# All experts for 512 tokens instead of 448, the fourth block's sums through one PSUM bank

## The chip, the cores and the metric

The kernel runs on one core of one Trainium2 chip. The time is device microseconds (us) of one execution; the figure for the kernel before is the median of 3 runs. The engines spoken of are PE (TensorE), DVE (VectorE), ACT (ScalarE), POOL (GpSimd, which here issues the gathering DMAs) and SP (SyncE, which issues all other DMAs).

## The reference, cut to what matters

One encoder layer for 1024 tokens of width 1024, all in float32: norm, two attentions, a merge, and then `peer`, a layer of 16384 one-neuron experts of which each token takes 16 in each of 8 heads. Only `peer` is touched by the change.

```python
s1 = jnp.einsum('thd,hnd->thn', q[:, :, 0], keys[:, 0])
s2 = jnp.einsum('thd,hnd->thn', q[:, :, 1], keys[:, 1])
v1, i1 = lax.top_k(s1, PEER_TOPK)          # 16 of 128
v2, i2 = lax.top_k(s2, PEER_TOPK)
cand = v1[..., :, None] + v2[..., None, :] # 256 sums, the best 16 are the token's experts
sc, ci = lax.top_k(cand, PEER_TOPK)
e = i1[ci // 16] * PEER_NKEYS + i2[ci % 16]
g = jax.nn.softmax(sc, axis=-1)
hid = jnp.einsum('thkd,td->thk', u[e], xb)
a = jax.nn.gelu(hid, approximate=False) * g
out = jnp.einsum('thk,thkd->td', a, v[e])
```

## The kernel before

The 1024 tokens are eight blocks of 128. Everything ahead of `peer` runs block by block on PE with its helpers: projections, attentions, `merge` (branches, output projection, residual, second norm, the scores q and the top 16 of each half, done by `top16` on DVE), and `choose` (the 16 best pairs of each head, on DVE with some copies on ACT).

The experts are computed in one of two ways. **Gathered**, for blocks 0, 1, the first half of 2, and 6, 7 (`GATHER`, function `experts`, L772 to L817): POOL issues for each of 128 choices of a token one indirect DMA that brings a row of u (128 tokens, 512 KB); DVE multiplies and sums it (L803); then the same with v, where DVE multiplies and adds (L809). Of the half block each token's 128 choices lie on two partitions, so that 64 + 64 DMAs do it instead of 128 + 128. **Dense**, for blocks 3, 4, 5 and the second half of 2 (`DENSE`, function `dense_experts`, L672 to L763): all 16384 experts at 448 tokens, in 128 chunks of 128 experts. The weight of an expert at a token, zero for nearly all, comes from `gates` (L633 to L670), which builds it on DVE, ACT and PE, four tokens a step, and writes it to DRAM, from where it is read back as `gj`.

In a chunk, PE makes `ph` (hidden values of 128 experts at 448 tokens) out of `ut` and the tokens `x2h`, `x2l`; float32 numbers are split into two float32r parts and multiplied in three products (`mm3`), so `ph` is 24 matmuls with 448 columns. ACT takes the Gelu, DVE multiplies by `gj` (L739), and `split` makes `ah`, `al` out of the first 384 tokens. One chunk later `second` adds up `v` times these: 18 matmuls with 512 columns into six PSUM banks, three blocks by two column halves, which stay open over all 128 chunks (L701). The half block goes unsplit, in plain float32, into a seventh bank: two matmuls (L704), which the profile lists as four. `ph` has the eighth bank. So all eight PSUM banks are taken.

What sets the order: the code emits instructions in a program order, and a scheduler that simulates the program gives each engine a fixed list. What is emitted early has priority. `experts` is emitted last, so gathers fill what is left, from block 0's choice on until the end. A tile pool that is opened in place of closed ones waits for all that was still at work in them. `fstack` is a stack of pools that closes before `dense_experts`; the pools `yza` and `tkp`, in which `choose` works, are not in it (L81, L82) and stay open to the end. The pool `dk` of the dense stage (L676) takes the room of the closed ones.

The last lines before the dense stage give its surroundings; `sel` runs `choose` for two blocks:

```python
    weave(mop(2, mp, yzb), 26, (gates(gk, d1), 32 * len(d1)))
    weave(mop(3, mp, yza), 26, (chain(sel([4, 5], yzb), gates(gk, d2)), 18 + 32 * len(d2)))
run(sel([6, 7], yza))
fstack.close()
dense_experts()
for seg in GATHER:
    experts(*seg)
```

## Time and profile before

| what | value |
|---|---|
| median of 3 runs | 3414.91 us (3405.22 to 3427.95) |
| span of the profiled execution | 3413.5 us, from its first to its last instruction; 1.4 us under the median |
| PE busy | 3029.9 us (89%) |
| DVE busy | 2723.6 us (80%) |
| ACT busy | 1395.7 us (41%) |
| POOL busy | 1377.9 us (40%) |
| moved by DMA | 1047 MB, mean 307 GB/s |
| dense stage, first to last matmul | about 2064 to 3374 us |

The profiled execution has only its span as its own time; what lies around it in a run (1.4 us against the median) is taken as unchanged. Shares of the span mix stages with different limits, so each stage is read by itself: by the busy time of the engines in a stretch, by the order of the instructions on an engine, and by the chain of waits (the work that ended last, followed back from the end, each step to what released it).

### The profile page before, as it was taken

How to read it: one execution, taken by the hardware profiler on the slowest of the kernel's cores; microseconds unless marked ns; L12 is line 12 of the kernel's file. 1: busy time of each engine (PE TensorE's matmuls, PEld its weight loads, DVE VectorE, ACT ScalarE, POOL GpSimd, SP SyncE). 2: the span in 40 equal slices, each digit the busy share in tenths (PEclk: the TensorE clock that was granted, in tenths of full speed). 3: DMA queues.
4: the chain of work that ended last, by engine and by line, in shares of the span. 5: the costliest groups of instructions: out<-in, count | busy, mean ns of one | idle time of the engine just before them, and what ended most of it. 6: DMA issues, size and time to landing. Idle time of an engine off the chain costs nothing.

```text
span 3413.5 us, 47714 instructions
## 1 busy us (share of the span) xinstructions
PE 3029.9 (89%) x15648; PEld 2435.4 (71%) x15648; DVE 2723.6 (80%) x5871; ACT 1395.7 (41%) x2959; POOL 1377.9 (40%) x1156
## 2 busy tenths in 40 slices
PE   7997689999979988888766658999999999999995
PEld 7986578888857656567655656777777777777774
DVE  4435798777759999988899898888788878788887
ACT  6633433443324554438505864333333333333332
POOL 0000445554534442343334421554444545445554
PEclk9998899999989988899887878999999999999997
DMA  7775989999989997788888877999999999999997
GB/s 240 215 243 169 357 313 356 345 330 337 323 322 350 329 321 233 227 281 309 328 288 303 319 250 242 347 339 333 329 336 333 333 340 329 331 332 329 330 331 269
DMA packets 415960, 1047.19 MB, mean 307 GB/s; under 512 B 44640, under 2 KB 181664, under 8 KB 413792
## 3 DMA queue, kind: packets, MB, share of 16 engines
q0 software_dynamic: 165888, 604.05, 50.3%
q1 hardware_dynamic: 249824, 440.09, 37.3%
q8 instruction: 123, 2.02, 0.2%
q14 instruction: 125, 1.02, 0.1%
HBM read 969.43 MB, written 73.96 MB: 306 GB/s over the span
## 4 chain that ended last, share of the span: by engine, by line
PE 69%; DVE 12%; DMA 7%; issue 6%; ACT 5%; POOL 1%; SPq 0%; DVEq 0%; ACTq 0%; POOLq 0%
PE ph L136 18%; PE mm L136 15%; PE acc L701 15%; PE mm L480 7%; PE sc L344 4%; PE acc L704 4%; PE pv L362 3%; PE tr L203 2%; DVE junk L803 2%; PE gg L660 2%; DVE acc L809 1%; DMA ge<-in_u_dram,ei 1%; ACT gst L662 1%; ACT o L652 1%; DMA wr<-in_w_bd_dram 1%
## 5 line engine op out<-in xcount | busy, mean ns | idle before, releaser
L797 POOL DMA_INDIRECT ge<-in_u_dram,ei x512 | 610.1, 1192 | 1051.0 <-DVE junk L803 415.2
L797 POOL DMA_INDIRECT ge<-in_v_dram,ei x512 | 626.1, 1223 | 695.3 <-DVE acc L809 446.3
L809 DVE SCALAR_TENSOR_TENSOR acc<-ge,a,acc 128x1024 f32<-128x1024 f32 x576 | 736.4, 1279 | 11.1 <-DMA ge<-in_v_dram,ei 5.1
L803 DVE SCALAR_TENSOR_TENSOR junk<-ge,xs 128x1024 bf16<-128x1024 f32 x576 | 701.6, 1218 | 40.2 <-DMA ge<-in_u_dram,ei 33.8
L129 DVE TENSOR_TENSOR wl<-wr,wh 128x1024 fp32r<-128x1024 f32 x232 | 283.8, 1224 | 322.0 <-ACT wh L128 196.4
L128 ACT CAST wh<-wr 128x1024 fp32r<-128x1024 f32 x232 | 243.3, 1049 | 605.8 <-PE ph L136 432.4
L136 PE MATMUL ph<-x2h,wh 128*128 128x448 f32 x1024 | 388.8, 380 | 11.3 <-DVE x2l L129 9.2
L136 PE MATMUL mm<-xh,wh 128*128 128x256 f32 (+1 forms) x1248 | 374.6, 326 | 5.4 <-ACT wh L128 3.8
L136 PE MATMUL mm<-xl,wh 128*128 128x256 f32 (+1 forms) x1248 | 369.5, 322 | 7.7 <-DVE xl L232 7.7
L136 PE MATMUL ph<-x2l,wh 128*128 128x448 f32 x1024 | 375.2, 366 | 0.0
L136 PEld LDWEIGHTS ph<-x2h,wh 128*128 128x128 f32 x1024 | 192.2, 188 | 128.5 <-issue 57.6
L136 PEld LDWEIGHTS mm<-xh,wh 128*128 128x128 f32 x1248 | 238.2, 191 | 30.5 <-ACT st L286 4.1
L136 PEld LDWEIGHTS mm<-xl,wh 128*128 128x128 f32 x1248 | 237.8, 191 | 29.3 <-DVE xl L232 9.7
L136 PE MATMUL mm<-xh,wl 128*128 128x256 f32 (+1 forms) x1248 | 239.3, 327 | 0.3 <-DVE wl L129 0.3
L344 PE MATMUL sc<-kt,qt 64*128 64x256 f32 (+3 forms) x608 | 215.9, 522 | 24.8 <-DVE mn L346 12.6
L136 PE MATMUL ph<-x2h,wl 128*128 128x448 f32 x1024 | 229.8, 366 | 0.0
L136 PEld LDWEIGHTS ph<-x2h,wl 128*128 128x128 f32 x1024 | 191.7, 187 | 17.5
L136 PEld LDWEIGHTS ph<-x2l,wh 128*128 128x128 f32 x1024 | 192.7, 188 | 15.7
L136 PEld LDWEIGHTS mm<-xh,wl 128*128 128x128 f32 x1248 | 186.4, 191 | 18.4 <-issue 1.5
L701 PE MATMUL acc<-vh,ah 128*128 128x512 f32 x768 | 197.6, 392 | 0.0
L701 PE MATMUL acc<-vh,al 128*128 128x512 f32 x768 | 194.9, 389 | 0.0
L701 PE MATMUL acc<-vl,ah 128*128 128x512 f32 x768 | 194.9, 389 | 0.0
(197 smaller groups left out, 5258.3 us busy)
## 6 DMA issues: line engine op xcount, KB each, us to landing
vr<-in_v_dram SPq DMA_DIRECT2D x128, 512.0 KB
wr<-in_ut_dram SPq DMA_DIRECT2D x128, 512.0 KB
wr<-in_w_in_dram SPq DMA_DIRECT2D x104, 512.0 KB
gdr<-gst SPq DMA_DIRECT2D x14, 2048.0 KB
gj<-gdr SPq DMA_DIRECT2D x448, 64.0 KB
wr<-in_w_bd_dram SPq DMA_DIRECT2D x40, 512.0 KB
wr<-in_w_out_dram SPq DMA_DIRECT2D x40, 512.0 KB
wr<-in_wq_dram SPq DMA_DIRECT2D x40, 512.0 KB
```

The source lines that it names most:

```text
L128: nc.scalar.copy(hi, raw)
L129: nc.vector.tensor_sub(lo, raw, hi.bitcast(F32))
L136: nc.tensor.matmul(o, w[a][:, k, :], xx[b][:, k, :], start=(i == 0), stop=(i == last))
L203: nc.tensor.transpose(o[:, i * P:(i + 1) * P], s, ident)
L344: nc.tensor.matmul(o[:, :k1 - k0], q, k[:, k0:k1], start=True, stop=True)
L362: nc.tensor.matmul(o[:, :P], aT[:, j - c, :], vt[:, v0 + j, :], start=(j == 0), stop=(j == n - 1))
L480: nc.tensor.matmul(o, w[:, k, :], xx[:, k, :], start=(k == 0), stop=(k == K - 1))
L701: nc.tensor.matmul(acc[i][hf], a[x][:, i * P:(i + 1) * P], b[y][:, hf * 512:hf * 512 + 512], **kw)
L704: nc.tensor.matmul(acc4[hf * n4:(hf + 1) * n4], ge[:, 3 * P:], vr[:, hf * 512:hf * 512 + 512], start=(j == 0), stop=(j == NCH - 1))
L797: nc.gpsimd.indirect_dma_start(out=t, out_offset=None, in_=src, in_offset=bass.IndirectOffsetOnAxis(ap=ei[:, k:k + 1], axis=0))
L803: nc.vector.scalar_tensor_tensor(junk, t, 1.0, xs, op0=OP.mult, op1=OP.mult, accum_out=hid[:, k:k + 1])
L809: nc.vector.scalar_tensor_tensor(acc, t, a[:, k:k + 1], acc, op0=OP.mult, op1=OP.add)
```

## The change

The half block 2 of the dense stage becomes a whole one: blocks 2, 3, 4, 5 are dense (512 tokens), blocks 0, 1, 6, 7 are gathered. The code that handled parts of blocks goes.

- The gathers of the first half of block 2, 64 of u and 64 of v, go, with their DVE instructions. `gates` gets 16 more steps (128 instead of 112) and takes block 2 ahead of block 3.
- `ph`, Gelu, the multiplication by `gj` and `split` take 512 columns; `gj` is 16 DMAs for four chunks instead of 14.
- The two float32 matmuls of the half block go. In their place `fourth` adds up the fourth block (block 5) in the split form: for two chunks at a time, six matmuls with 512 columns for one column half in one PSUM bank (`acc3`), then an addition on DVE into `rest` in SBUF, which began as the block's residual. The other half uses the same bank, after `second` of the newer chunk. So every second chunk has on PE: `ph`, `fourth(0)`, `second`, `fourth(1)`; the others `ph`, `second`.
- Buffers: `vh`, `vl`, `ah`, `al` have 4 (of 3), `vr` 2 (of 3), `ge` 2 (of 3).
- The pools `yza` and `tkp` move into `fstack`, at the same place; so their room is given to `dk`.
- At the end, the residual of the third dense block is loaded into a buffer of `vr`.

Comments that the change only removes, and lines that follow from the new names, are left out:

```diff
--- before.py
+++ after.py
...
-DENSE = [(3, 0, 128), (4, 0, 128), (5, 0, 128), (2, 64, 128)]
-GATHER = [(0, 0, 128), (1, 0, 128), (2, 0, 64), (6, 0, 128), (7, 0, 128)]
-ND = len(DENSE)
-DT = sum(b - a for _, a, b in DENSE)
...
-VBUFS = 3
+DBLK = [2, 3, 4, 5]
+SBLK = [0, 1, 6, 7]
+ND = len(DBLK)
+DT = ND * P
+VBUFS = 4
+RBUFS = 2
+ABUFS = 4
...
-    yza = ctx.enter_context(tc.tile_pool(name="yza", bufs=1))
-    tkp = ctx.enter_context(tc.tile_pool(name="tkp", bufs=1))
...
     fstack = ExitStack()
+    yza = fstack.enter_context(tc.tile_pool(name="yza", bufs=1))
+    tkp = fstack.enter_context(tc.tile_pool(name="tkp", bufs=1))
...
-            b, ta, tb = DENSE[k0]
-            it4 = dsel[b]
-            for t in range(ta, tb, 4):
+            it4 = dsel[DBLK[k0]]
+            for t in range(0, P, 4):
...
-            # the last, half block: its two column halves lie on the two halves of a bank's partitions
-            acc4 = pd.tile([P, 512], F32, name="acc4") if n4 else None
-
-            def second(j, a, b, ge, vr):
+            rest = dk.tile([P, D], F32, name="rest", bufs=1)
+            nc.sync.dma_start(rest, hd[DBLK[3]])
+
+            def second(j, a, b):
                 for x, y in ((0, 0), (0, 1), (1, 0)):
                     kw = dict(start=(j == 0 and x == y), stop=(j == NCH - 1 and x == 1))
                     for i in range(3):
                         for hf in range(2):
                             nc.tensor.matmul(acc[i][hf], a[x][:, i * P:(i + 1) * P], b[y][:, hf * 512:hf * 512 + 512], **kw)
-                if n4:
-                    for hf in range(2):
-                        nc.tensor.matmul(acc4[hf * n4:(hf + 1) * n4], ge[:, 3 * P:], vr[:, hf * 512:hf * 512 + 512],
-                                         start=(j == 0), stop=(j == NCH - 1))
+
+            def fourth(hf, chunks):
+                o = pd.tile([P, 512], F32, name="acc3", tag="acc3")
+                cs = slice(hf * 512, hf * 512 + 512)
+                todo = [(a[x], b[y]) for _, a, b in chunks for x, y in ((0, 0), (0, 1), (1, 0))]
+                for n, (aa, bb) in enumerate(todo):
+                    nc.tensor.matmul(o, aa[:, 3 * P:4 * P], bb[:, cs], start=(n == 0), stop=(n == len(todo) - 1))
+                nc.vector.tensor_add(rest[:, cs], rest[:, cs], o)
+
+            def sums(chunks):
+
+                two = len(chunks) == 2
+                if two:
+                    fourth(0, chunks)
+                second(*chunks[-1])
+                if two:
+                    fourth(1, chunks)
+                    chunks.clear()
...
-                vr = dk.tile([P, D], F32, name="vr", tag="vr", bufs=VBUFS)
+                vr = dk.tile([P, D], F32, name="vr", tag="vr", bufs=RBUFS)
...
-                ge = dk.tile([P, T], F32, name="ge", tag="ge", bufs=VBUFS)
+                ge = dk.tile([P, T], F32, name="ge", tag="ge")
...
-                ah = dk.tile([P, 3 * P], F32R, name="ah", tag="ah", bufs=VBUFS)
-                al = dk.tile([P, 3 * P], F32R, name="al", tag="al", bufs=VBUFS)
-                split(ge[:, :3 * P], ah, al)
-                if late:
-                    second(*late)
-                late = (j, (ah, al), (vh, vl), ge, vr)
-            second(*late)
...
+                ah = dk.tile([P, T], F32R, name="ah", tag="ah", bufs=ABUFS)
+                al = dk.tile([P, T], F32R, name="al", tag="al", bufs=ABUFS)
+                split(ge, ah, al)
+                if new:
+                    chunks.append(new)
+                    sums(chunks)
+                new = (j, (ah, al), (vh, vl))
+            chunks.append(new)
+            sums(chunks)
+            for i, b in enumerate(DBLK):
+                hx = rest
                 if i < 3:
+                    if i < 2:
+                        hx = hxs[i]
+                    else:
+                        hx = dk.tile([P, D], F32, name="hx", tag="vr", bufs=RBUFS)
+                        nc.sync.dma_start(hx, hd[b])
...
-    def experts(b, ta, tb):
+    def experts(b):
...
-    for seg in GATHER:
-        experts(*seg)
+    for b in SBLK:
+        experts(b)
```

## Rows read from the trace of the kernel before

**Rows 1.** Stretches: us; PE, PEld, DVE, ACT, POOL busy; clock; DMA share; GB/s.

```profile
1660.00:1770.00 110.00, 74.23 (x353) 60.13 (x353) 108.09 (x490) 22.14 (x55) 29.11 (x30) 0.86 0.85 299
...
1960.00:2034.00 74.00, 48.51 (x280) 42.19 (x278) 74.00 (x300) 49.76 (x113) 16.26 (x16) 0.79 0.70 245
...
2064.00:3373.00 1309.00, 1306.88 (x5883) 1023.60 (x5884) 1072.93 (x1535) 423.34 (x671) 636.02 (x503) 1.00 0.93 326
```

**Rows 2.** Line 803 alone by stretch, 1660 to 2064: us, DVE busy (two records each).

```profile
1660.00:1770.00 110.00, 33.06 (x55) 0.86 0.85 299
...
sum 404.00, DVE 78.09; mean DVE 13.02
```

**Rows 3.** Line 809 alone by stretch: us, DVE busy, clock, DMA share, GB/s.

```profile
1820.00:1960.00 140.00, 48.13 (x38) 0.77 0.86 307
1960.00:2034.00 74.00, 19.34 (x16) 0.79 0.70 245
```

**Rows 4.** Chain of waits by line: 1660 to 1770, 1770 to 1820, 1820 to 1960.

```profile
by line: DVE junk L803 23.7%; issue 13.4%; DVE qs L551 7.5%; DVE iu L550 7.4%; DVE iu L553 6.9%; DVE vv L549 5.6%; DVE vv L552 5.6%; DVE ci L550 3.4%; DVE cand L551 3.3%; DVE ci L553 3.2%; DVE sv L552 2.7%; DVE sv L549 2.6%; DVE o L644 2.2%
by line: PE mm L480 32.5%; DMA wr<-in_w_out_dram 18.6%; DMA wr<-in_w_bc_dram 13.1%; DMA ge<-in_u_dram,e 11.4%; DVE junk L803 7.2%; issue 6.6%; POOL ge L797 3.1%; DVE o L654 3.0%; DVE o L644 2.5%; DVE ohib L607 0.7%; SPq L504 0.7%; PE tr L20
by line: PE gg L660 29.7%; PE mm L480 23.1%; ACT gst L662 14.3%; ACT o L652 8.8%; issue 5.5%; ACT sq L651 4.6%; PE tr L203 3.2%; DVE xs L520 1.8%; PE sc L537 1.8%; ACT xs L518 0.9%; ACT L805 0.9%; ACT L116 0.9%; DVE junk L803 0.9%; DVE acc 
```

**Rows 5.** Timeline of PE, one chunk of the dense stage: start, us, instruction.

```profile
2501.63 0.47 PE L136 MATMUL ph<-x2h,wh 128*128 128x448 f32 x1
2501.94 0.37 PE L136 MATMUL ph<-x2l,wh 128*128 128x448 f32 x1
...
2506.64 1.54 PE L701 MATMUL acc<-vh,ah 128*128 128x512 f32 x6
...
2509.38 1.52 PE L701 MATMUL acc<-vh,al 128*128 128x512 f32 x6
2510.83 1.08 PE L704 MATMUL acc<-vr,ge 128*64 128x512 f32 x4
2511.84 0.47 PE L136 MATMUL ph<-x2h,wh 128*128 128x448 f32 x1
```

**Rows 6.** Timeline of PE, a place where ph follows line 701 directly.

```profile
2092.34 1.56 PE L701 MATMUL acc<-vh,al 128*128 128x512 f32 x6
2093.74 0.37 PE L136 MATMUL ph<-x2h,wh 128*128 128x448 f32 x1
```

**Rows 7.** Timelines of DVE, SP and PE where the dense stage begins.

```profile
2033.91 0.27 DVE L553 FIND_INDEX8 iu<-vv,qs 128x8 uint32<-128x128 f32 x1
...
2034.25 0.34 SPq L708 DMA_DIRECT2D wfd<-in_wf_dram  x1
...
2064.10 0.74 PE L136 MATMUL ph<-x2h,wh 128*128 128x448 f32 x1 [9.24 <-DVE x2l L129]
```

**Rows 8.** Timeline of DVE, pieces of choose for block 6.

```profile
2035.29 1.49 DVE L549 MAX8 sv<-cand 128x8 f32<-128x112 f32 x8
...
2100.40 0.21 DVE L609 TENSOR_TENSOR sel<-ohib 128x64 f32<-128x64 bf16 x1
...
2103.77 0.22 DVE L609 TENSOR_TENSOR sel<-ohib 128x64 f32<-128x64 bf16 x1
```

**Rows 9.** Waits, 2113 to 3320: us in total, times, longest us.

```profile
ACT ah L128 <- DVE ge L739: 212.1, 109, 4.8
```

**Rows 10.** Timelines of PE and DVE at the end.

```profile
3372.95 1.52 PE L701 MATMUL acc<-vh,al 128*128 128x512 f32 x6
...
3400.58 2.60 DVE L809 SCALAR_TENSOR_TENSOR acc<-ge,a,acc 128x1024 f32<-128x1024 f32 x2
...
3408.35 1.27 DVE L769 SCALAR_TENSOR_TENSOR hx<-hx,nr,wfd 64x1024 f32<-64x1024 f32 x1
```

**Rows 11.** Line 754 (DVE, PSUM bank added to SBUF): ns min/median/max.

```profile
L754 DVE TENSOR_TENSOR hx<-hx,acc x6: 677/679/686, 3373.4 to 3394.4; 128x512 f32<-128x512 f32 x6
```

**Rows 12.** Line 644 alone (one per gates step), 1800 to 2014: DVE busy.

```profile
1800.00:2014.00 214.00, 43.50 (x64) 0.79 0.79 285
```

More of the change, by code (lines that the diff above doesn't have):

```diff
@@ L31 @@
 GROUPS = [[0, 1], [2, 3, 4, 5, 6, 7]]
-DENSE = [(3, 0, 128), (4, 0, 128), (5, 0, 128), (2, 64, 128)]
-GATHER = [(0, 0, 128), (1, 0, 128), (2, 0, 64), (6, 0, 128), (7, 0, 128)]
-ND = len(DENSE)
-DT = sum(b - a for _, a, b in DENSE)
-DOFF = [sum(b - a for _, a, b in DENSE[:i]) for i in range(len(DENSE))]
-DBLK = [d[0] for d in DENSE]
-SBLK = [d[0] for d in GATHER]
-VBUFS = 3
+DBLK = [2, 3, 4, 5]
[5 more added lines that the diff above has]
+ABUFS = 4
 TB = 32
@@ L655, in gates, with later @@
                                                 op0=OP.is_equal, op1=OP.mult)
-                def later(n=DOFF[k0] + t - ta, t=t, o1=o1, o2=o2, gst=gst):
+                def later(n=k0 * P + t, t=t, o1=o1, o2=o2, gst=gst):
                     o = psp.tile([P, 512], F32, name="gg", tag="tr")
@@ L680, in dense_experts @@
             with tc.tile_pool(name="dps0", bufs=2, space=PSUM) as pt:
[L681 to L682 removed]
+                for i, b in enumerate(DBLK):
                     xs = wp.tile([P, KC, P], F32, name="xd", tag="wr", bufs=WBUFS).rearrange("p a b -> p (a b)")
[L684 removed]
+                    nc.sync.dma_start(xs, xn2d[b])
                     for g in range(2):
@@ L709, in dense_experts @@
             hxs = []
-            late = None
+            chunks = []
+            new = None
             for j in range(NCH):
                 if j == NCH - 2:
-                    for i, (b, ta, tb) in enumerate(DENSE):
+                    for b in DBLK[:2]:
                         hx = dk.tile([P, D], F32, name="hx", tag="hx", bufs=2)
-                        if i < 3:
-                            nc.sync.dma_start(hx, hd[b])
-                        else:
-                            n = tb - ta
-                            hx = hx[:2 * n, :512]
-                            for hf in range(2):
-                                nc.sync.dma_start(hx[hf * n:(hf + 1) * n], hd[b][ta:tb, hf * 512:(hf + 1) * 512])
+                        nc.sync.dma_start(hx, hd[b])
                         hxs.append(hx)
                 uw = wtile(ut[j])
-                vr = dk.tile([P, D], F32, name="vr", tag="vr", bufs=VBUFS)
+                vr = dk.tile([P, D], F32, name="vr", tag="vr", bufs=RBUFS)
                 nc.sync.dma_start(vr, v[j * P:(j + 1) * P, :])
@@ L754, in dense_experts @@
                         nc.vector.tensor_add(dst, dst, acc[i][hf])
-                else:
-                    h4 = hx
-                    hx = dk.tile([P, D], F32, name="hx", tag="vr", bufs=VBUFS)[:n]
-                    nc.vector.tensor_add(h4, h4, acc4[:2 * n])
-                    for hf in range(2):
-                        nc.sync.dma_start(hx[:, hf * 512:(hf + 1) * 512], h4[hf * n:(hf + 1) * n])
-                sq = wp.tile([P, KC, P], F32, name="sq", tag="wr", bufs=WBUFS).rearrange("p a b -> p (a b)")[:n]
-                final(hx, sq, smd, b * P + ta, wfb)
+                sq = wp.tile([P, KC, P], F32, name="sq", tag="wr", bufs=WBUFS).rearrange("p a b -> p (a b)")
+                final(hx, sq, smd, b * P, wfb)
     def final(acc, sq, pool, t0, wfb):
@@ L809, in experts @@
             nc.vector.scalar_tensor_tensor(acc, t, a[:, k:k + 1], acc, op0=OP.mult, op1=OP.add)
-        for i in range(1, parts):
-            nc.sync.dma_start(xs[:n], acc[i * n:(i + 1) * n])
-            nc.vector.tensor_add(acc[:n], acc[:n], xs[:n])
         wfb = gp.tile([P, D], F32, name="wfb", tag="ge")
         nc.sync.dma_start(wfb, wf.to_broadcast([P, D]))
-        final(acc[:n], junk[:n], sms, b * P + ta, wfb)
+        final(acc, junk, sms, b * P, wfb)
     dn = [None, None]
```

34 lines of the change are left out of this document (9 added, 25 removed).

## The prediction

> **What bounds the kernel now.** I read the busy times by stretch first. From 2064 to 3373 us PE is busy for 1306.9 of 1309 us, at a granted clock of 1.00, the upper of its two levels (2.4 GHz) [rows 1]: the dense stage is 128 chunks of PE work, and whatever lengthens a chunk there lengthens the kernel. DVE has 1073 of the 1309 us, and DMA a share of 0.93, so the gathers of blocks 6 and 7 fill these two nearly as well. The end shows that both finish almost together: the last matmul at 3374, the last gathered row added at 3403, the last instruction at 3408, the span's end at 3413.5 [rows 10].
>
> Before the dense stage it is otherwise. From 1660 to 1770 DVE is busy for 108 of 110 us and PE for 74; from 1960 to 2034 DVE for 74 of 74 [rows 1]. The chain of waits says the same of the first stretch: its largest share, 23.7%, is line 803, the gathers of the half block 2 [rows 4]. From 1820 to 1960 the chain goes through the matmuls of the gates and of the merge and the copies of ACT, and line 803 has 0.9% of it [rows 4]: DVE has work there that nobody waits for. So the change takes gathers out of a place where some of their DVE time counts, and puts matmuls into a place where all of it counts.
>
> **The chunk.** One chunk takes 2511.84 - 2501.63 = 10.21 us: 24 matmuls of `ph` 5.01, the 18 of line 701 4.19 (0.233 each), the half block 1.01 [rows 5]. With 512 columns `ph` grows to 5.01 x 512/448 = 5.73, `fourth` puts in 12 matmuls for two chunks, so 6 x 0.233 = 1.40 for each, and 1.01 goes: 5.73 + 4.19 + 1.40 = 11.32, or 1.11 more. That is the upper bound. It leaves out that the float32 matmuls of line 704 also cost something at their borders: the first `ph` behind them takes 0.31 to the next one, where the other 23 take (2506.64 - 2501.94)/23 = 0.204, and the last six of line 701 ahead of them take 1.45, where the twelve before take 1.37 for six [rows 5]. Where `ph` stands directly behind line 701, the six there take 1.40 [rows 6]. The change has no float32 matmul left in the chunk, so I take 0.10 and 0.09 off: (5.01 - 0.10) x 512/448 = 5.61, and 4.10, and 1.37, together 11.08. That is 0.87 more, and 128 x 0.87 = **111 us**. Bounds 105 and 142.
>
> **The wait on the bank.** `fourth(1)` may not start before DVE has added `fourth(0)`'s sums out of the bank. What lies between on PE is `second`, 4.1 us. The addition takes 0.68 us (line 754 is the same operation) [rows 11], so DVE may be up to 3.4 us late. How late DVE is shows where ACT waits for line 739: 212.1 us in 109 times, 1.9 each, the longest 4.8, with 0.6 of the operation itself in it [rows 9]. So DVE is 1.3 us late on average and 4.2 at worst, and few of the 64 pairs stall. `fourth(0)` of the next pair has two `ph` as cover. I take **5 us**, bounds 0 and 30. Here a wait joins a full engine: if the addition is late, PE stands, and all behind it (`fourth(1)`, the next `ph`), while DVE goes on with gathers. The Trainium skill (TensorE: Matmul & The Clock Gate, section "A second HAM failure mode: psum-queue depth-cycling") speaks against such a change: a kernel that cycled PSUM banks in each iteration left PE idle for moments between groups of matmuls, and its clock went up and down. No run here shows that yet; the row shows 1.00 and 2 us of idle in 1309.
>
> DVE gets 0.68 more in each chunk, and 512 columns in place of 448 and of 384 in two operations, about 0.26 by columns; 128 x 0.94 = 120 us, so 1193 of some 1420 us, 84% instead of 82%. The 14% more of `gj` and the two buffers of `vr` cost nothing I can see: a `vr` has over 10 us to land, and the DMA load of a chunk is spread over 11.1 instead of 10.2 us. If that cover fails, `second` waits and the second rival comes.
>
> **What goes before the dense stage.** The gathers of block 2 are 78 us of line 803 [rows 2] and 67 us of line 809 up to 2034 [rows 3]. What comes back is read by stretch.
> From 1660 to 1770: 33 us of line 803 [rows 2], all on an engine that is full. But 16 more gates steps come in, each 0.68 us for line 644 [rows 12] and about 0.6 for two of line 654, some 20 us, and I expect them here and not earlier, for they are woven to the end of the merge. Net 13; bounds 0 and 33.
> From 1770 to 1820: gathers are 7.2 + 11.4 + 3.1 = 21.7% of the chain's 50 us, 11 us; the loads of w_out and w_bc, 31.7% or 16 us, compete with gathers, and I give half of that back [rows 4]. Together 19; bounds 11 and 27.
> From 1820 to 1960: PE and ACT pace it; 5, bounds 0 and 15.
> From 1960 to 2034: 19 us of line 809 [rows 3] on a full DVE, but ACT has gates to copy until about 2014; 16, bounds 12 and 19.
> Sum **-53 us**. Both ends: 94 if every bound is the upper. At the lower, 23, less what the gates steps would cost if they paced the merge (they come at about 3 us each in the trace, 16 x 3 = 48), so nothing at all.
>
> **The pools that move.** This is the edit that looks like nothing. In the kernel before, the dense stage opens while `choose` is still at work on blocks 6 and 7: the last `top16` of the merge ends at 2034.1, and SP issues the first load into `dk` at 2034.25 [rows 7], while `choose` for block 6 only begins. The first `ph` comes 30 us later, at 2064.1 [rows 7]. With `yza` and `tkp` under `dk`, the stage opens only when `choose` is through with block 7. Alone, `choose` searches with five operations of eight rounds of 1.5 us [rows 8], with their small loads 9 us, and then has four rounds of 3.4 us (from one `sel` to the next, 2103.77 - 2100.40) [rows 8], 13.5; with the rest some 26 us. Block 7's search fits beside block 6's rounds, so both take about 48 us. Then the tokens are transposed and split, eight steps of about 1.7 us, 14. So the first `ph` comes 62 us after the merge instead of 30: **+32 us**, bounds 18 and 55. Behind the waiting load, SP holds back `vr`, `gj` and further `ut`; behind the first `x2h` copy ACT holds back all splits. POOL isn't held: block 6's gathers start earlier against the dense stage than before.
>
> **The end.** The gathers that remain are the same 512, from about 2113 to 3403, 1290 us; the dense stage becomes 128 x 11.08 = 1418 us and they begin ahead of it, so they are done before PE. After the last matmul there remain seven additions (4.8 us), the norm, the scaling and the store, which took 3413.5 - 3403.2 = 10 us [rows 10], and some 2 us for four blocks in turn: 17 instead of 39. **-22 us**; bounds 0 and -27.
>
> **Sum.** 3413.5 - 53 + 32 + 111 + 5 - 22 = 3486.5 us of span. The median of the runs is 1.4 above the span, so **3488 us**, 2.1% slower.
>
> **Rivals.** *More comes back ahead of the dense stage.* If each of the 145 us of gathers up to 2034 counts, because the gates and the merge go faster as soon as DVE answers at once, less 20 for the gates steps: 3413.5 - 125 + 32 + 111 + 5 - 22 = 3414.5, no change (3416 as a run). For it: DVE is full in two stretches. Against it: the chain from 1820 to 1960. It turns to faster only if also the opening of the dense stage costs nothing: 3384; with the chunk at its lower bound 3378, the other side. The point from which that decides is a return of about 160 us, opening included.
> *The bank or DVE becomes the bound.* If the addition stands 1 to 3 us too late in each pair, because DVE's fixed list has gathers ahead of it: 64 to 192 us more, 3550 to 3680. For it: one bank, and DVE at 84%. Against it: 1.9 us of wait against 4.1 of cover. If the clock also fell to the lower level, half, for the 24 matmuls behind each stall, each would take its 0.204 [rows 5] twice: 24 x 0.204 x 64 = 313 us more, about 3800.
> *The pools don't delay the stage.* If the room under `dk` is free anyway, 32 less: 3456. That is within the forecast's range.
>
> **Chances.** The forecast 0.62 (own range 3450 to 3530), more comes back 0.20, faster by that way 0.07, the bank or DVE 0.11. Slower by over 1% (above 3449), 0.72: the forecast but for a small part, and the bank. Within 1% 0.21. Faster 0.07. 1% is about what a measurement of this kernel can tell, since its three runs lie 0.7% apart. The range reaches from 3410, which takes in the first rival, to 3560, with the chunk's upper bound and a part of the second.
>
> **What would show it.** A chunk pair of about 22.2 us in the timeline of PE, PE busy throughout and its clock at 1.00; no line 803 or 809 between about 1665 and the dense stage; a gap on PE of some 60 to 70 us ahead of the first 512-column `ph`, with `choose` in it alone; the last gathered row some 100 us ahead of the last matmul. The forecast is wrong if a pair takes clearly more than 22.6 us, with idle on PE ahead of `fourth`, or if the dense stage starts earlier than 1990 or later than 2110.

## The result and the profile after

The changed kernel takes 3446.3 us (median of 4 runs, 3443.5 to 3450.4), the kernel before in the same session 3414.5 us (3405.2 to 3428.0). The ratio is 1.0096, with a 95% interval from 1.0069 to 1.0123: about 1% slower, where 2.1% had been forecast. The profiled execution has a span of 3443.9 us against 3413.5, 30.4 more. The sum behind the forecast had 73.

The stretches of the kernel after, in the columns of [rows 1] (us; PE, PEld, DVE, ACT, POOL busy; clock; DMA share; GB/s):

```profile
1660.00:1770.00 110.00, 95.87 (x496) 82.08 (x493) 107.17 (x509) 59.58 (x137) 0.00 (x0) 0.92 0.51 174
1770.00:1940.00 170.00, 139.59 (x827) 121.34 (x826) 116.02 (x463) 152.93 (x356) 0.00 (x0) 0.89 0.41 154
1940.00:2033.00 93.00, 6.20 (x25) 4.87 (x26) 78.50 (x259) 17.48 (x29) 39.05 (x32) 0.50 0.66 232
2100.00:3200.00 1100.00, 1100.00 (x4855) 910.84 (x4854) 988.51 (x1281) 343.07 (x519) 585.00 (x460) 1.00 0.96 343
3200.00:3428.00 228.00, 228.00 (x1008) 188.79 (x1007) 92.16 (x126) 69.67 (x106) 0.00 (x0) 1.00 0.33 103
```

POOL does nothing between 1660 and 1940: the gathers of block 2 are gone. From 1940 to 2033 PE has 6 us of work; that is the wait for the dense stage. From 2100 to 3428 PE is busy throughout at a clock of 1.00, and from 3200 on POOL issues no gather any more.

Where the dense stage begins, the answer to [rows 7]: timelines of DVE (the merge's last search), SP (the first loads into `dk`) and PE of the kernel after; columns start us, us, instruction, in brackets the idle time before it.

```profile
1938.36 0.27 DVE L552 FIND_INDEX8 iu<-vv,qs 128x8 uint32<-128x128 f32 x1
...
2013.40 0.32 SPq L692 DMA_DIRECT2D rest<-hd  x1
2013.77 0.42 SPq L720 DMA_DIRECT2D wfd<-in_wf_dram  x1
...
1938.10 1.09 PE L686 MATMUL trd<-ident,xd 128*128 128x128 f32 x8 [1.12 <-ACT gst L660]
2015.14 1.97 PE L686 MATMUL trd<-ident,xd 128*128 128x128 f32 x8 [75.95 <-DVE x2l L126]
...
2032.70 0.79 PE L133 MATMUL ph<-x2h,wh 128*128 128x512 f32 x1 [9.47 <-ACT wh L125]
```

The merge ends at 1938.6 instead of 2034.2, 95.6 earlier. Then 94.1 us pass until the first `ph`, instead of 29.9. Together the first `ph` comes 31.4 us earlier.

Not all of the 95.6 us comes from the change. In each of the last two merges SP loads `keyT` once. The first of these loads lies ahead of every gathered row of block 2 (in the kernel before, none reaches DVE until 1670), and it too is 10.3 us earlier. The loads in the kernel before and after (number, ns min/median/max, first and last start):

```profile
L504 SPq DMA_DIRECT2D keyT<-in_keyst_dram x2: 327/328/328, 1553.2 to 1784.0; - x2
```

```profile
L503 SPq DMA_DIRECT2D keyT<-in_keyst_dram x2: 328/330/333, 1542.9 to 1760.4; - x2
```

From the first load to the end of the merge it is 481.0 us before and 395.7 after, **85.3** less: 13.3 up to the second load, 72.0 behind it.

One chunk, the answer to [rows 5] (timeline of PE):

```profile
2512.20 1.98 PE L133 MATMUL ph<-x2h,wl 128*128 128x512 f32 x8
2514.02 0.39 PE L706 MATMUL acc<-vh,ah 128*128 128x512 f32 x1
...
2514.70 1.52 PE L699 MATMUL acc<-vh,ah 128*128 128x512 f32 x6
2516.06 1.52 PE L699 MATMUL acc<-vl,ah 128*128 128x512 f32 x6
2517.42 1.52 PE L699 MATMUL acc<-vh,al 128*128 128x512 f32 x6
2518.78 0.39 PE L133 MATMUL ph<-x2h,wh 128*128 128x512 f32 x1
```

Every matmul of 512 columns, `ph` or not, follows the one before after 0.2266 us: (2514.02 - 2512.20)/8, and 1.36 for six of L699. The stretches say the same: 4855 matmuls in 1100 us, 48 to a chunk, are 10.88 a chunk, a pair 21.8. (Some expectations below say 10.84; that came from the 443 in a stretch of 100 us, where matmuls cut at both edges count whole.) `fourth` (L706) doesn't stand where the code has it: the scheduler put one half of it inside a `ph` and parted the other, three matmuls here ahead of `second`. The dense stage takes 3428.8 - 2032.7 = 1396.1 us instead of 1310.4, 85.7 more.

The end, the answer to [rows 10] (timelines of DVE for the last gathered row, of PE, of DVE):

```profile
3203.95 1.28 DVE L805 SCALAR_TENSOR_TENSOR acc<-ge,a,acc 128x1024 f32<-128x1024 f32 x1
...
3428.39 0.39 PE L706 MATMUL acc<-vh,al 128*128 128x512 f32 x1
...
3438.48 1.28 DVE L776 SCALAR_TENSOR_TENSOR rest<-rest,nr,wfd 128x1024 f32<-128x1024 f32 x1
```

From the last matmul to the span's end 15.1 us instead of 39.0: 23.9 less. So -10.3 - 85.3 + 64.2 + 85.7 - 23.9 = 30.4, the whole difference of the two profiled executions; by the medians it is 31.8. Against the forecast's -53, +32, +116 (111 and 5 for the bank) and -22, three terms are off by 30 to 32 us each, and with different signs; the -10.3 belongs to none of them.

### The profile page after: what moved, and what is told of

Its sections match the earlier page's. It is cut to its first block, busy times and chain, and to the rows that moved or that the text cites. A ratio compares the mean times of both kernels' runs of the same rounds, so it can differ in the third digit from the quotient of the medians.

```text
span 3443.9 us, 48357 instructions
## 1 busy us (share of the span) xinstructions
PE 3112.2 (90%) x16032; PEld 2567.9 (75%) x16032; DVE 2700.0 (78%) x5848; ACT 1445.3 (42%) x3029; POOL 1245.7 (36%) x1028
## 4 chain that ended last, share of the span: by engine, by line
PE 73%; issue 14%; DVE 5%; DMA 4%; ACT 3%; POOL 1%; SPq 0%; DVEq 0%; ACTq 0%; POOLq 0%
PE ph L133 20%; PE mm L133 17%; PE acc L699 15%; PE mm L479 5%; PE acc L706 5%; PE sc L343 4%; PE pv L361 3%; PE tr L202 2%; DVE junk L799 1%; POOL ge L793 1%; DMA ge<-in_u_dram,ei 1%; DVE p L345 1%; DVE acc L805 1%; DMA g<-gd 0%; DMA ge<-in_v_dram,ei 0%
## 5 line engine op out<-in xcount | busy, mean ns | idle before, releaser
L793 POOL DMA_INDIRECT ge<-in_u_dram,ei x512 | 624.1, 1219 | 1283.8 <-DVE ei L628 677.4
L805 DVE SCALAR_TENSOR_TENSOR acc<-ge,a,acc 128x1024 f32<-128x1024 f32 x512 | 655.2, 1280 | 17.0 <-DMA ge<-in_v_dram,ei 9.5
L799 DVE SCALAR_TENSOR_TENSOR junk<-ge,xs 128x1024 bf16<-128x1024 f32 x512 | 623.9, 1218 | 46.7 <-DMA ge<-in_u_dram,ei 36.8
L133 PE MATMUL ph<-x2h,wh 128*128 128x512 f32 x1024 | 399.4, 390 | 11.0 <-ACT wh L125 9.5
L133 PE MATMUL ph<-x2l,wh 128*128 128x512 f32 x1024 | 399.1, 390 | 0.0
L133 PEld LDWEIGHTS mm<-xh,wh 128*128 128x128 f32 x1248 | 237.8, 191 | 29.9 <-ACT wh L125 4.0
L133 PE MATMUL ph<-x2h,wl 128*128 128x512 f32 x1024 | 253.2, 389 | 0.0
L125 ACT CAST vh<-vr 128x512 fp32r<-128x512 f32 x256 | 140.4, 619 | 262.9 <-PE acc L706 223.2
L125 ACT CAST ah<-ge 128x512 fp32r<-128x512 f32 x128 | 79.6, 622 | 288.5 <-DVE ge L746 275.7
L699 PE MATMUL acc<-vh,ah 128*128 128x512 f32 x768 | 198.1, 389 | 0.0
```

The lines of the kernel that those rows point to most:

```text
L125: nc.scalar.copy(hi, raw)
L133: nc.tensor.matmul(o, w[a][:, k, :], xx[b][:, k, :], start=(i == 0), stop=(i == last))
L699: nc.tensor.matmul(acc[i][hf], a[x][:, i * P:(i + 1) * P], b[y][:, hf * 512:hf * 512 + 512], **kw)
L793: nc.gpsimd.indirect_dma_start(out=t, out_offset=None, in_=src, in_offset=bass.IndirectOffsetOnAxis(ap=ei[:, k:k + 1], axis=0))
L799: nc.vector.scalar_tensor_tensor(junk, t, 1.0, xs, op0=OP.mult, op1=OP.mult, accum_out=hid[:, k:k + 1])
L805: nc.vector.scalar_tensor_tensor(acc, t, a[:, k:k + 1], acc, op0=OP.mult, op1=OP.add)
```

## The experiments

One caution on single stretches: the profiled executions of the kernel before and of three versions of it that leave the front alone (below) end their merge at 2034.2, 2027.0, 2025.4 and 2023.5, those of the changed kernel and the versions with its front at 1936.2 to 1948.3. Most of this spread is there already at the first load of `keyT`, which lies between 1539.1 and 1553.2 in all versions, with and without the gathers of block 2. From that load to the end of the merge the two groups take 478.5 to 481.0 and 395.4 to 397.5 us. So moments ahead of the dense stage can differ by 10 us and more between any two runs, while distances from that load are good to 2 or 3 us, and the sizes below are taken from it.

Theory after the result: the gathers cost far more ahead of the dense stage than the chain of waits showed; the opening waits for `choose`, and `choose` is held up by gathers; the chunk is shorter because something about the matmuls of `ph` changed. The rival in each case is the step of the prediction.

**What the gathers and the gates steps cost.**

```diff
 for seg in GATHER:
-    experts(*seg)
+    if seg[0] != 2:
+        experts(*seg)          # the kernel before; 64 rows get hd alone
...
```

> The kernel before without the gathers of half block 2 (its 64 output rows are then the residual alone: the expert sum and the final norm of these rows are left out). Everything else stands, float32 half block included. The prediction's step (gathers ahead of the dense stage cost 53 us): the merge's last top-16 comes at about 1981 instead of 2034.1, the time falls by 53 us there and by up to 28 at the end, because the gathers then end ahead of the last matmul: about 3335. Theory after the result (they cost 96 us there, nearly all of it after 1784, because DVE work that the chain of waits hardly shows delays PE all the same): merge end at 1935 to 1945, time about 3290 to 3300.

Measured: 3299.1 us, ratio 0.969 (0.966 to 0.972); the last search, where the kernel before has it at 2033.91:

```profile
1918.85 0.29 DVE L553 FIND_INDEX8 iu<-vv,qs 128x8 uint32<-128x128 f32 x1
```

Its loads of `keyT`:

```profile
L504 SPq DMA_DIRECT2D keyT<-in_keyst_dram x2: 327/328/328, 1541.5 to 1740.2; - x2
```

The merge ends 115.0 us earlier than in the kernel before, but 11.7 of these are there at the first load. So the gathers delayed the merge by 103.3 us, of the 145 us of DVE time that they have there [rows 2, 3]. That is near the theory's 96, which was read off moments. The prediction's 53 has 20 us of gates steps taken off, which stay out here as well; its sum for the gathers alone is 73. Up to the second load the gathers cost 32.1 us (230.8 against 198.7), about the 33 that the prediction gave to its first stretch; so "nearly all of it after 1784" fell. Where the rest went shows a comparison from the second load to the last search, 1784.0 to 2034.0 in the kernel before and 1740.2 to 1918.85 without the gathers:

```profile
1784.00:2034.00 250.00, 165.02 (x878) 142.91 (x877) 230.16 (x619) 170.12 (x386) 97.33 (x84) 0.78 0.82 294
```

```profile
1740.20:1918.85 178.65, 147.73 (x869) 128.55 (x868) 128.44 (x489) 164.38 (x381) 0.00 (x0) 0.91 0.42 156
```

The same work on PE (878 and 869 records) and on ACT (170 and 164 us) takes 71 us less once DVE has 102 us less to do. PE's gaps shrink by 54 us, and its matmuls by 17, at a granted clock of 0.91 instead of 0.78. The prediction had given this part 40 us (19, 5 and 16), because from 1820 to 1960 the chain runs mostly through PE and ACT [rows 4].

```diff
-            for t in range(0, P, 4):
+            for t in range(64 if k0 == 0 else 0, P, 4):     # the changed kernel
...
```

> The changed kernel with 48 instead of 64 gates steps ahead of the merge of blocks 4 and 5: the first 64 tokens of block 2 get no weights of their own (the dense stage reads other tokens' in their place), everything else stands. Without the gathers of the half block the kernel before ended its merge 120.7 us earlier (1913.4 against 2034.1), the changed kernel only 96 us earlier (1938). Theory: the 16 more gates steps are the difference; merge end at about 1913, first ph 25 us earlier, time about 3421. Rival (PE and ACT take the steps in their gaps): merge end at 1930 or later, time within 8 us.

Measured: 3431.3 us in one run, span 3429.5. The 1913.4 in this expectation was misread, the start of a group of searches; the right number is 1918.85.

```profile
1924.86 0.29 DVE L552 FIND_INDEX8 iu<-vv,qs 128x8 uint32<-128x128 f32 x1
```

Its loads of `keyT`:

```profile
L503 SPq DMA_DIRECT2D keyT<-in_keyst_dram x2: 327/330/332, 1544.9 to 1746.5; - x2
```

From the first load to the end of the merge it is 380.2 us, 15.5 less than in the changed kernel, all of it up to the second load; the first `ph` comes 15.1 earlier, the span is 14.4 shorter. So the 16 steps are on the path, at 15.5 us (the prediction had 20, in the same stretch). The theory's 25 us came from the misread number. 103.3 - 15.5 = 87.8 against 85.3 in the changed kernel.

**What the opening waits for.**

```diff
-    for b in SBLK:
+    for b in (0, 1, 7, 6):
```

> The changed kernel with one edit: the gathers of block 7 are issued ahead of block 6's, so that no gathered row can reach DVE before choose of block 7 has ended. Theory: 22 gathered rows of block 6 (L799, 22 x 1.30 us and 6.2 us of waits on DVE, 34.8 us in all) lie inside choose of block 7 and hold up the opening of the dense stage's SBUF; without them the first load of the dense stage goes at about 1979 instead of 2013.4, the first ph at about 1998 instead of 2032.7, the time is about 35 us lower (3411). Gathers start some 10 us later and end about 3215, still 200 us ahead of the last matmul. Rival (choose itself takes 75 us, or the opening waits for something else): first ph at 2025 or later, time within 8 us of the changed kernel's.

Measured: 3433.9 us, ratio to the kernel before 1.0077 (1.0051 to 1.0103). That is 12.4 us less than the changed kernel by the medians, and the two intervals overlap; the profiled execution was the fastest of its four, with a span of 3423.8, 20 less. What the edit does to the opening is read from the trace. Timelines of DVE, SP and PE:

```profile
1941.62 0.29 DVE L552 FIND_INDEX8 iu<-vv,qs 128x8 uint32<-128x128 f32 x1
...
1989.11 0.32 SPq L692 DMA_DIRECT2D rest<-hd  x1
...
2007.58 0.80 PE L133 MATMUL ph<-x2h,wh 128*128 128x512 f32 x1 [6.58 <-ACT wh L125]
```

Both calls of `choose`, undisturbed, hold the pool for 47.2 us after the merge, and the first `ph` comes 65.7 after it: the prediction's 48 and 62. In the changed kernel it was 94.1. The other 28 us are the gathers of block 6, which start as soon as that block is chosen. (5 us of the gain are lost again in the dense stage, 1401.1 us instead of 1396.1; why is not shown.) Groups by line of DVE in the changed kernel, 1965 to 2014 (busy us, mean ns, then idle time before them):

```profile
L799 DVE SCALAR_TENSOR_TENSOR junk<-ge,xs 128x1024 bf16<-128x1024 f32 x22 | 26.9, 1222 | 6.2 <-DMA ge<-in_u_dram,ei 6.0
L606 DVE TENSOR_TENSOR ohib<-ohib 128x512 bf16<-128x512 bf16 (+2 forms) x18 | 5.6, 313 | 0.3
```

Most of the short operations of `choose` for block 7 (as L606, 0.3 us) have a gathered row (L799, 1.2 us) ahead of them. The theory's 35 us for the first `ph` were 10 too many (25.1): this run's merge ends 3.3 us later, and it took `choose` alone at 40 us.

```diff
+    yza = ctx.enter_context(tc.tile_pool(name="yza", bufs=1))    # as before, not in fstack
+    tkp = ctx.enter_context(tc.tile_pool(name="tkp", bufs=1))
...
-VBUFS = 4
+VBUFS = 3                     # and hx in the buffers of vr, for room
...
-ABUFS = 4
+ABUFS = 3
```

> The changed kernel with the pools yza and tkp opened as in the kernel before (outside the stack that closes ahead of the dense stage); to make room, vh, vl, ah, al have three buffers instead of four and the residual rows hx take vr's buffers. Theory: the move of the pools costs 94 - 30 = 64 us at the opening; first ph at about 1938 + 30 = 1968, choose then runs beside the first chunks without slowing them (as in the kernel before), a chunk still takes 10.84 us, time 3446 - 64 = about 3382. Rival 1 (the work of choose only moves, and the first ten chunks become DVE's): first ph at 1968 but the 20th chunk's no more than 20 us earlier than in the changed kernel; time 3425 to 3440. Rival 2 (three buffers are too few): chunk over 11.0 us, time over 3446.

Measured: 3414.5 us, ratio 1.0016 (1.0000 to 1.0032). The first `ph` stands at 1969.79, 27.3 after the merge and 62.9 earlier than in the changed kernel, as the theory has it. But the span is only 31.5 less, for two reasons. The third `hx` is loaded after the last matmul, so the end takes 24 us instead of 15. And each chunk is longer. PE's timeline, from the first `ph` to the last matmul:

```profile
1969.79 0.80 PE L135 MATMUL ph<-x2h,wh 128*128 128x512 f32 x1 [6.11 <-DVE x2l L128]
...
2514.37 2.03 PE L135 MATMUL ph<-x2h,wl 128*128 128x512 f32 x8
2516.24 1.52 PE L699 MATMUL acc<-vh,ah 128*128 128x512 f32 x6
2517.60 1.52 PE L699 MATMUL acc<-vl,ah 128*128 128x512 f32 x6
...
3388.45 0.39 PE L706 MATMUL acc<-vh,al 128*128 128x512 f32 x1
```

Eight `ph` take 1.87 us, 0.233 each, while L699 is at 1.36 for six as it was. From the first `ph` to the last matmul (3388.8) it is 1419 us, 23 more than in the changed kernel: -62.9 + 23 + 8.5 = -31.4. It isn't rival 1, a bound on DVE, which would leave gaps on PE, and there are none from 2000 on. Three buffers (rival 2) would leave gaps too; what lengthens the matmuls themselves is shown further below.

> Both edits: pools as in the kernel before and block 7's gathers first. Theory: once the dense stage no longer waits for choose, the order of the gathers is worth nothing at the opening: first ph at about 1968 as with the pools alone, time within 5 us of that run (about 3382). If the two gains added (another 35 us), what the gathers delay would not be choose but the split of x2 or the first chunks.

Measured, with both edits: 3417.0 us, ratio 1.0022 (1.0007 to 1.0037), first `ph` at 1967.0: as with the pools alone. So the gathers of block 6 cost time at the opening only while `choose` has to end before the stage opens.

**Why `ph` was faster in the changed kernel.** The program fixes each tile's place in SBUF, and the moved pools moved `x2h` from 112256 to 89696 (bytes in a partition), while `wh`, the stationary operand, went from 83040 to 81504.

```diff
-        gs = pt([P, H], "gs")
+        gs = pt([P, 2 * H], "gs")[:, :H]       # 32 bytes more in tkp: x2h 32 further
```

> The run with the pools as before, and one number changed: a small tile of tkp is 32 bytes longer, so that x2h and every later tile of the dense stage begin 32 bytes further on. In the changed kernel x2h lies at 89696 and wh at 81504 (both 32 over a multiple of 64) and a 512-column ph takes 0.2267 us; with the pools back x2h lies at 110720 (a multiple of 64), wh still at 81504, and the same instruction took 0.2333. Theory: the pitch of ph hangs on where x2 lies against 64 bytes, by chance moved by the change; then ph is back at 0.2267, a chunk at 10.84 to 10.88 instead of 11.01 us, time 3414 - 128 x 0.16 = about 3394. Rival: the pitch comes from something else in that run (three buffers, the neighbours of x2 in SBUF, DVE's reads): ph stays at 0.2333 and the time at 3410 to 3420.

> The changed kernel with a constant tile 32 bytes longer, which moves all tiles behind it, wh and x2h both: both then begin at a multiple of 64. Theory A (what counts is that moving operand and stationary operand lie alike): ph stays at 0.2267, chunk 10.84, time as the changed kernel's. Theory B (a moving operand at a multiple of 64 is slower where each matmul also loads new weights): ph 0.2333, chunk 11.0, time about +22.

> The run with the pools as before and the same constant tile 32 bytes longer: wh at a multiple of 64, x2h 32 over one. Theory A (they must lie alike): ph 0.2333, time 3410 to 3420. Theory B (the moving operand alone counts): ph 0.2267, about 3394.

> The run with the pools as before, x2h moved on by 96 bytes (110816; against wh at 81504 the distance is then a multiple of 128, as in the changed kernel and in the run with every tile moved), and the residual row of the third block in a buffer of its own, loaded two chunks ahead. Theory: the pitch of a 512-column ph goes by the distance of x2h and wh: 0.2267 at a multiple of 128, 0.2287 at 64 over one, 0.2333 at 32 over a multiple of 64. So ph at 0.2267, chunk 10.84, last matmul at 1970 + 1388 = about 3360, tail 16 instead of 23, time about 3380: below both kernels (ratio to the kernel before about 0.991). Rival (three buffers or x2's neighbours give the rest): chunk 10.90 as with 32 bytes, time about 3395.

> The run with the pools as before and the third residual row in its own buffer, x2h now 480 bytes further on than with the pools back (111200, wh at 81504: the distance is 58 x 512). So far a 512-column ph took 0.2266 at a distance of 8192 (two runs, both ends moved alike in one), 0.2332 at 29216 (two runs, likewise), 0.2291 at 29248 and 0.2327 at 29312; a multiple of 128 isn't enough. Theory: the distance within 512 bytes (one row of a weight tile) decides, and 0 is the fast one: ph 0.2266, chunk 10.84, last matmul at about 3365, time about 3382. Rival 1 (it is the place in SBUF or the larger distance): ph 0.2290 to 0.2333, time 3395 to 3410.

> The same with x2h at 110944, a distance 256 over a multiple of 512. If the distance within 512 bytes decides: a pitch of its own between 0.2266 and 0.2333, at 512 bytes the fast one. If only the place in SBUF decides: 0.2290 to 0.2333 here and at 512 as well.

> The same with x2h at 114272, a distance of 32768, four times that of the changed kernel. If a larger power of two than 512 decides: ph 0.2266 here and not at 29696. If 512 decides: 0.2266 in both. If the place in SBUF decides: slow in both.

> The changed kernel with one unused tile of 32 bytes ahead of x2h: wh stays at 81504, x2h goes from 89696 to 89728, a distance 32 over a multiple of 512 as with the pools back and in the kernel before. Nothing else changes. Theory: ph 0.2333 instead of 0.2266, chunk 11.0 instead of 10.84, time about 20 us higher: so much of the prediction's 111 us the moved pools gave back by chance. Rival (the distance isn't it; x2's place in SBUF or the three buffers are): ph 0.2266, time within 8 us.

The edits of the others are of the same kind: another length of `gs` (both_128, both_256, both_512, both_8192, which also give the third `hx` a buffer of its own), `cst` 32 bytes longer, which moves `wh` and `x2h` alike (all_0, wh0_x32), and in the changed kernel itself:

```diff
+            gap = dk.tile([P, 8], F32, name="gap", bufs=1)
             xh = dk.tile([P, KC, T], F32R, name="x2h", bufs=1)
```

Measured. The pitch is the mean distance between the starts of successive `ph` matmuls from 2500 to 2620 us in PE's timeline, some 250 of them; the records are those of PE from 2600 to 2700 us.

| run | x2h - wh | over a multiple of 256 | pitch, us | records in 100 us | span, us |
|---|---|---|---|---|---|
| changed kernel | 8192 | 0 | 0.2266 | 443 | 3443.9 |
| all_0 | 8192 | 0 | 0.2267 | 443 | 3453.5 |
| both_256 | 29440 | 0 | 0.2266 | 443 | 3382.4 |
| both_512 | 29696 | 0 | 0.2266 | 443 | 3383.7 |
| both_8192 | 32768 | 0 | 0.2268 | 443 | 3383.7 |
| pools_back | 29216 | 32 | 0.2331 | 436 | 3412.4 |
| wh0_x32 | 29216 | 32 | 0.2331 | 437 | 3420.9 |
| after_x32 | 8224 | 32 | 0.2330 | 436 | 3470.0 |
| pools_back_32 | 29248 | 64 | 0.2291 | 440 | 3404.8 |
| both_128 | 29312 | 128 | 0.2328 | 436 | 3401.7 |

Two rows of the stretches, the changed kernel and the same with `x2h` 32 bytes further on:

```profile
2600.00:2700.00 100.00, 100.00 (x443) 82.81 (x442) 86.95 (x136) 32.93 (x50) 52.94 (x42) 1.00 0.96 348
```

```profile
2600.00:2700.00 100.00, 100.00 (x436) 81.37 (x435) 85.81 (x131) 36.11 (x56) 49.47 (x40) 1.00 0.93 335
```

Moving both operands alike leaves the pitch as it was (all_0 against the changed kernel, wh0_x32 against pools_back); moving one by 32 bytes changes it. So it is the distance of the two, not the place. (The span of all_0 is 9.6 us above the changed kernel's, but all of that lies ahead of its first `ph`, 7.9 of it ahead of the first load of `keyT`.) In these edits all tiles of `dk` behind `x2h` move with it; L699, both of whose operands are among them, keeps its pitch. That they must lie alike against 64 bytes fell with pools_back_32, that a multiple of 128 is enough with both_128. A multiple of 256 gave the fast pitch each time, and both_256 shows that a whole row of 512 bytes isn't needed. pools_back_32 has a ratio of 0.9966 (0.9946 to 0.9985), both_128 of 1.0007 (0.9990 to 1.0024). after_x32 costs 26 us: 21 in the dense stage, which by the pitches is 128 x 24 x 0.0064 = 20, and its first `ph` is 5.3 later.

both_512 is the best version: 3385.3 us, ratio to the kernel before 0.9915 (0.9883 to 0.9947). Its first and last matmul:

```profile
1968.95 0.79 PE L135 MATMUL ph<-x2h,wh 128*128 128x512 f32 x1 [6.11 <-DVE x2l L128]
...
3368.17 0.39 PE L706 MATMUL acc<-vh,al 128*128 128x512 f32 x1
```

It has the 512 dense tokens and the rotating bank of the change, but the pools where they were, three buffers, the third `hx` loaded early, and `x2h` a multiple of 256 from `wh`; its median is 61 us under the changed kernel's.

**The same in the kernel before.** Its distance is 29216, the slow one.

> The kernel before with one tile of tkp 96 bytes longer, so that x2h lies a multiple of 128 from wh (112352 and 83040; as it was, 32 over a multiple of 64). Theory: a 448-column ph falls from about 0.2045 to 0.2267 x 448/512 = 0.198, a chunk from 10.21 to about 10.06 us, PE's last matmul comes 20 us earlier; the time stays within 5 us, because the gathers end the kernel. Rival (at 448 columns the distance doesn't count, or 0.2045 is already the faster pitch): chunk 10.21.

> The kernel before with x2h 480 bytes further on (112736, wh at 83040: 58 x 512 apart instead of 32 over a multiple of 512). Theory: what the prediction scaled by columns was the slow pitch; at the fast distance a 448-column ph takes 0.2266 x 448/512 = 0.198 (or 0.200, if what a matmul takes on top of its columns is the same 13 ns) instead of 0.2045, a chunk 10.06 to 10.10 instead of 10.21, the last matmul comes 14 to 19 us earlier. The time changes by less than 8 us, because the gathers end the kernel. Rival: 0.2045 is the pitch of 448 columns at any distance.

Measured: before_128 ratio 1.0003 (0.9987 to 1.0020), before_512 0.9976 (0.9957 to 0.9995). With 448 columns the pitch is 0.2041 as it was, 0.2033 at 128 over and 0.2027 at 0. So the theory of a pitch by columns fell here: the fast distance gains 0.0014 a matmul, 4 us in the dense stage (1310.4 to 1306.3), not 14 to 19. The other 9 us of before_512's profiled run lie ahead of its first `ph` (2055.35 against 2064.10); before_128, at a slower distance, has 2051.7, so that is no effect of the distance that these runs show.

**The float32 matmuls.**

```diff
-                if n4:
+                if n4 and j in (0, NCH - 1):           # the kernel before
```

> The kernel before without the float32 matmuls of the dense half block in all chunks but the first and last (the sums of 64 rows are left out). The prediction gave them 1.01 us a chunk and another 0.10 + 0.09 us at their borders with the float32r matmuls. If the borders cost that: a chunk takes 24 x 0.2045 + 18 x 0.2267 = 8.99 us instead of 10.21. If the borders cost nothing: 9.18. In time: the gathers cannot go faster with the transfers of a chunk closer together, so the end is theirs: PE's last matmul 125 to 155 us earlier, the time itself falls by less than 60.

Measured: 3403.5 us in one run; PE's last matmul comes 151 us earlier, as expected. The stretch from 2100 to 3200 has 5085 records, 42 to a chunk: 9.09 us, between the two expectations. About half of the borders' 0.2 us is there. The rest can't be told, since `ph`'s pitch also went from 0.2041 to 0.2066 with the same addresses, which is not explained. The time hardly falls, since the gathers end this kernel.

**The bank.**

```diff
-                two = len(chunks) == 2
+                two = True                             # the changed kernel
```

> The changed kernel with the fourth block's sums taken chunk by chunk: the bank is emptied twice in every chunk instead of twice in two, 128 more additions of 0.68 us on DVE. The prediction's rival (one bank, DVE late): PE stands 1 to 3 us ahead of fourth in many chunks, time up by 64 us or more. Theory after the result (the matmuls of fourth stand inside the next ph, so the bank has far more than the additions need; DVE at 78% has room): chunk 10.84 to 10.90, time within 10 us of the changed kernel's 3446.

Measured: 3512.2 us in one run, span 3510.5, 66.6 more than the changed kernel. The theory was wrong: with twice the additions, the time rises by what the prediction's rival gives, though not by the wait that it names. The stretches (columns as above), then PE's waits from 2100 to 3200 (us in total, times, longest us), then PE's timeline at the end:

```profile
2300.00:2400.00 100.00, 96.55 (x420) 77.76 (x419) 95.87 (x106) 28.61 (x44) 50.91 (x44) 1.00 0.96 341
3000.00:3100.00 100.00, 95.75 (x414) 76.77 (x413) 96.93 (x106) 28.05 (x44) 55.25 (x46) 1.00 0.97 349
...
3480.00:3490.00 10.00, 5.64 (x22) 3.51 (x20) 5.18 (x10) 6.45 (x18) 0.00 (x0) 0.88 0.00 1
3490.00:3502.00 12.00, 6.59 (x12) 3.32 (x12) 6.24 (x8) 1.27 (x6) 0.00 (x0) 0.50 0.32 131
```

```profile
PE acc L699 <- ACT vh L125: 14.9, 18, 1.0
PE acc L699 <- ACT ah L125: 7.8, 8, 1.0
PE acc L699 <- DVE vl L126: 6.6, 12, 1.2
...
PE acc L706 <- DVE rest L707: 0.3, 1, 0.3
```

```profile
3497.86 0.79 PE L706 MATMUL acc<-vh,ah 128*128 128x512 f32 x1 [0.78 <-DVE rest L707]
3498.45 0.63 PE L706 MATMUL acc<-vl,ah 128*128 128x512 f32 x1
3498.88 0.63 PE L706 MATMUL acc<-vh,al 128*128 128x512 f32 x1
3500.28 0.79 PE L706 MATMUL acc<-vh,ah 128*128 128x512 f32 x1 [0.78 <-DVE rest L707]
```

DVE has 96 of 100 us, and PE stands for 3 to 4 of 100. But it hardly stands before the bank (0.3 us in all): it stands before `second`, whose operands ACT and DVE split too late. The last rounds of `fourth` stand alone at the end of PE's list: after 3483 PE stands 1.9, 0.8 and 4.7 us for additions, the clock goes to 0.88 and then 0.50, the lower level, and a round of three matmuls then takes 2.43 us, 0.78 of it a wait. The dense stage is 70.5 us longer (1466.6 against 1396.1), what follows it 6.5 shorter. Between 2100 and 3200 PE is idle for 34.6 us (1065.4 of 1100 busy), and its 4617 matmuls there would take 1046 of the busy 1065 us at 0.2266, so some 19 go to matmuls that follow each other more slowly; at the end it waits 11.3 us for the bank. So what "two chunks at a time" saves is above all DVE's time.

## Why the prediction was wrong

Its sum was 73 us, the difference 30.4. The five terms, with what the runs gave them:

- **The return of the gathers, -53; measured -85.3.** The step that failed is the reading of the stretches from 1770 to the end of the merge by the chain of waits: 19 + 5 + 16 = 40 us, where 72.0 came back. The chain names what came last at each moment, here mostly the gates' and the merge's matmuls and ACT's copies, and so the stretch from 1820 to 1960 got 5 us [rows 4]. Without the gathers the same matmuls come closer together and run at a higher clock (0.91 instead of 0.78). The first stretch, where DVE was full, was right: 13 in the text, 13.3 measured, made of about 32 for the gathers less about 16 for the gates steps. The rival "more comes back" had the mechanism of the missing part, but its size was no better: of the 145 us that it counts in full, 103.3 come back, and its 125 us are 40 too many where the forecast's 53 are 32 too few.
- **The opening, +32; measured +64.2.** The mechanism is shown, and the size of `choose` too: 47.2 and 65.7 where nothing disturbs it, 48 and 62 in the text. What failed is the sentence on POOL. It says that block 6's gathers start earlier, and puts at nothing that their rows go through DVE, where `choose` for block 7 now is on the path. That is 28 of the 32 us missing, and the gap wasn't filled by `choose` alone, as the text wanted to see.
- **The chunk, +111; measured 85.7.** A chunk is 10.88, not 11.08. The term of `ph` is the one mis-sized: 5.61 in the text, 24 x 0.2266 = 5.44 in the trace. At the old distance of `x2h` and `wh` it is 24 x 0.2331 = 5.59, and the dense stage of after_x32 is 1416.9 us, +106.5. So scaling by columns came out for the operands where they were. It is no rule, though: at the fast distance it would give 0.2027 x 512/448 = 0.2317, and 0.2266 was measured. That moving two pools would also move `x2h` to where `ph` runs faster wasn't foreseen, and the trace of before, with one distance only, couldn't show it. The other 4 us are `second` and `fourth`, at 0.2266 a matmul and not 0.228.
- **The bank, +5; measured nothing.** PE is busy for 1100.00 of 1100 us; the scheduler gave the bank more cover than `second` alone. In the chunk shown above, the three matmuls at 2514.02 complete one half's sums and end by 2514.70, and the bank is used next at 2521.72, 7.0 us later instead of 4.1. The rival is real at twice the additions (66.6 us), through DVE more than through the bank. In the kernel after, the row that answers to [rows 9] has a longer mean wait (2.4 us against 1.9) and a shorter longest one (4.2 against 4.8); first PE's next use of the bank, then ACT's wait:

```profile
2521.72 0.39 PE L706 MATMUL acc<-vh,ah 128*128 128x512 f32 x1
```

```profile
ACT ah L125 <- DVE ge L746: 250.8, 104, 4.2
```

The rule of the Trainium skill cited in the prediction (TensorE: Matmul & The Clock Gate, section "A second HAM failure mode: psum-queue depth-cycling") did not show in the changed kernel: the bank rotates, PE has no gap from 2100 to 3428, and the clock stays at 1.00. The end of one_chunk bears on it: there the bank alone sets the pace, PE stands before each round, and the clock is 0.50. That it would also rise again between rounds no run shows.

- **The end, -22; measured -23.9.** Right. The last gathered row comes 224 us ahead of the last matmul, not 100: the gathers began at 1972 and ran for 1233 us.

The misses are -32.3, +32.2, -25.3, -5 and -1.9 us, and -10.3 us are the earlier front, which the change didn't make and no term covers: together -42.6. That the first two cancel is chance, and so the time says little about the mechanism; three of the five steps were wrong in size. Whether the medians hold such a difference of the fronts too isn't known, since each kernel was profiled once. The rival "the pools don't delay the stage" fell: with the pools back it opens 62.9 us earlier.

## What to carry to other kernels

When an engine is relieved of work in a stretch where it is full, expect most of that time back, even where the chain of waits names others: here 32 of 33 us came back in one stretch and 71 of 102 in the next, and DVE had been busy for nine tenths of both. Look at the clock of the stretch, which may rise with the gaps gone. To compare two traces, measure from a common event ahead of the change; here 10 of 96 us lay ahead of it. When a pool moves under a closed stack, list everything that can now stand on the path of the last user of that memory, other queues' work on the same engine included. And after any change of the SBUF layout, compare the pitch of unchanged matmuls; here 32 bytes were worth 20 us.

## What the runs showed of the hardware

A 512-column float32r matmul that reloads its weights each time follows the one before after 0.2266 us when its moving operand lies a multiple of 256 bytes from its stationary one (8192, 29440, 29696 and 32768 bytes), after 0.2291 at 64 over, 0.2328 at 128 over and 0.2331 at 32 over. Other distances were not run. With 448 columns the difference is smaller, 0.2027 to 0.2041, and the distance isn't all there: in no_acc4 the pitch is 0.2066 at the old one. The operands of L699 lie a multiple of 256 apart in the changed kernel and in pools_back, since every tile of `dk` has such a size, and their pitch is 0.2267 in both. What in the chip makes it so no run shows.
